# The Mamba stage of a hybrid backbone: GpSimd subtracts a weight tile in four operations instead of one

## The chip, the cores and the metric

One core of a Trainium2 chip runs the kernel. Its engines have queues of their own, worked in order: TensorE (PE; its weight loads are shown apart, as PEld), VectorE (DVE), ScalarE (ACT), GpSimd (POOL) and SyncE (SP), which here issues most transfers. The metric is the time of one execution on the device, in microseconds (us). It was 2333.77 us in the median of three runs (2329.89 to 2337.48).

## The reference

Two layers of a backbone over 512 latent tokens and 256 context tokens of width 1024, all in float32. Layer 0 mixes by differential attention and RWKV-7, layer 1 by a bidirectional Mamba-2; each is followed by a ConvFFN. The change lies in layer 1:

```python
def mamba_inputs(h, w_in, conv_w, conv_b):
    p = h @ w_in
    z, xbc, dt = jnp.split(p, [SSM_INNER, SSM_INNER + SSM_CONV_CH], axis=-1)
    xbc = jax.nn.silu(dwconv_centred(xbc, conv_w, conv_b))
    xs, bm, cm = jnp.split(xbc, [SSM_INNER, SSM_INNER + SSM_GROUPS * SSM_STATE], axis=-1)

def odd_mixer(...):
    for d in range(2):                       # forwards and backwards
        h_ctx_final = ssd_state(...)         # the context's state
        yl, _ = ssd_scan(..., h_ctx_final)   # in chunks of 128 tokens
        y_l = y_l + (jnp.flip(yl, axis=1) if d == 1 else yl)
    o_lat = mamba_out(y_l, z_l, norm_w, w_out)   # gate, group norm, @ w_out
```

## The kernel before

A matrix product is made with three matmuls, on operands split into a high and a low half: with `w = wh + wl` and `x = xh + xl`, PE adds up `wh*xh`, `wh*xl` and `wl*xh`. Activations are split once; weights are split as they come. A weight tile is 128 x 1024 values: SP loads it into `ws`, ScalarE copies it to `wh` in PE's format, and another engine forms `wl = ws - wh`. In most stages that engine is DVE (L150); in the Mamba stage it is POOL (`wsplit_g`, L1349), 52 times. `ws`, `wh` and `wl` have two buffers each.

`dense_stream` (L1433) makes the products of the stage item by item: `item_z`, `item_x`, `item_b`, `item_c` with 8 blocks of 128 inputs each, and `item_o` (the output projection) with 4 blocks of 256 columns. `mm_half` (L1408) makes one half of an item's matmuls, into a PSUM tile `dps`; between the halves the next item is split and the one after it loaded, so a tile is split half an item to an item ahead of its use. After the first half of the next item the result is taken out of PSUM (`evac`): for x, b and c the convolution's five taps and SiLU (`conv_silu`, tiles `cv`, `xf`, `bf`, `cf`), for z a SiLU (`sz`), for o the addition to `xl`. ScalarE and DVE do that.

In turn with the dense stream, `scan(u)` (L1568) makes the recurrence for 4 heads at a time, `u` from 0 to 7. DVE forms the weighted inputs `xw`, which PE multiplies (L1615, L1628) into chunk states `hst`. For each head a tile `bc` with the running sums of the decay is loaded, in ScalarE's queue; POOL masks it with two selects (`mask_bc`, L1557), ScalarE takes the exponential, DVE adds the two directions and multiplies by `cb` (`bc<-bc`, `bc<-bc,cb`), and PE multiplies the result with the inputs (L1668). `fin` (L1671) puts the parts together on DVE (`th`, `gy`) and sums the squares for the group norm in `sqs`, on POOL or DVE by turns (L1686); PE adds these up over partitions (L1732). Before the scans, `dt_chain` (L1453) prepares step sizes and decays from [128, 384] tiles (`e_`, `z`, `dg`).

The framework sets each engine's order from the order of the code, with the results' way out of PSUM raised in priority; it puts the waits in, from what each operation reads and writes.

Of the kernel before, what the change touches and what calls it, by code (L numbers as in the profile page):

```python
# [8 lines left out]
F32 = mybir.dt.float32  # L9
# [116 lines left out]
def build(tc, a, out, dump=None, stop=None):  # L126
    nc = tc.nc
    V, S, G, PE, SY = nc.vector, nc.scalar, nc.gpsimd, nc.tensor, nc.sync
# [4 lines left out]
    def act(o, i, func, bias=0.0, scale=1.0, **kw):  # L133
        S.activation(out=o, in_=i, func=func, bias=bias, scale=scale, **kw)  # L134
# [18 lines left out]
    MUL, ADD, SUB, MAX, MIN = ALU.mult, ALU.add, ALU.subtract, ALU.max, ALU.min  # L153

    with ExitStack() as es:
# [34 lines left out]
        def wload(src, k, m):  # L190
            w = wsp.tile([128, 8, 128], F32, tag="ws", name="ws", bufs=WB[0])
            SY.dma_start(out=w[:, 0:k, 0:m], in_=src.rearrange("(k p) m -> p k m", p=128))
            return w[:, 0:k, 0:m]
# [163 lines left out]
        with ExitStack() as e0:  # L357
# [11 lines left out]
            with ExitStack() as e1:  # L369
# [3 lines left out]
                with tc.tile_pool(name="px", bufs=1) as px:  # L373
# [14 lines left out]
                    for k0 in range(0, KD, 2):  # L388
# [5 lines left out]
                        if k0 in FW:  # L394
                            for m in FW[k0]:
                                w = wload(a["ev_w_in"][:, m * 128:(m + 1) * 128], KD, 128)
# [160 lines left out]
                for j in JA:  # L557
                    q = j // 4
# [713 lines left out]
        with ExitStack() as e3:  # L1272
# [50 lines left out]
            with ExitStack() as e:  # L1323
# [19 lines left out]
                def wsplit_g(w):  # L1343
                    hi = wsp.tile([128, 8, 128], F32R, tag="wh", name="wh", bufs=2)
                    lo = wsp.tile([128, 8, 128], F32R, tag="wl", name="wl", bufs=2)
                    hi = hi.rearrange("p k m -> p (k m)").rearrange("p (k m) -> p k m", m=w.shape[-1])
                    lo = lo.rearrange("p k m -> p (k m)").rearrange("p (k m) -> p k m", m=w.shape[-1])
                    act(hi, w, AF.Copy)
                    G.tensor_tensor(out=lo, in0=w, in1=hi.bitcast(F32), op=SUB)  # L1349
                    return hi, lo  # L1350

                def wload_g(src, k, m):
# [75 lines left out]
                def split_item(it):  # L1428
                    if it is not None and "w" not in it:
                        load_item(it)  # L1430
                        it["w"] = wsplit_g(it["raw"])
# [462 lines left out]
```

## Time and profile before

The profile is of one execution, of 2334.5 us around a span of 2332.8 us. A window of the trace gives the time in which each engine was busy in a stretch; PE's clock is the share of full speed that was granted.

| stretch | length | PE | DVE | ACT | POOL | PE's clock |
|---|---|---|---|---|---|---|
| whole span | 2332.8 us | 2165.8 | 1398.6 | 989.7 | 390.9 | 0.97 |
| up to the stage, 0 to 1400 us | 1400.0 us | 1296.4 | 781.8 | 601.7 | 184.1 | 0.96 |
| the Mamba stage, 1400 to 1935 us | 535.0 us | 487.1 | 423.6 | 253.3 | 189.7 | 0.97 |
| after it | 397.8 us | 382.3 | 193.1 | 134.7 | 17.2 | 0.99 |

A row of the timeline gives the start in the span, the length, the engine, the line, the operation with the tile that it writes and those that it reads, and in brackets the idle time of the engine before it and what ended it. A row of the waits gives the total, the number and the longest. A row of the groups gives count, busy time and mean length in ns, then the idle time before.

### The profile page before, as it was taken

To read this page: it belongs to the slowest core of one execution; us is meant where nothing else is said; L and a number is where in the kernel's file an instruction comes from. 1 tells how busy PE (TensorE), PEld (TensorE's weight loads), DVE (VectorE), ACT (ScalarE), POOL (GpSimd) and SP (SyncE) were. 2 spreads that over 40 slices of the span, in tenths; PEclk is the share of its full clock that TensorE was granted. 3 is DMA by queue.
4 is the path that set the end of the run, shared out by engine and by line. 5 is a ranking of instruction groups with operands and counts; after the bars stand their busy time and mean duration, and the time that the engine had idled before them with its cause. 6 is when DMAs were issued, how large, how long until landed. Compare 5 with 4: busy or idle time off the path is not lost. (4 is left out here: it accounts for less than half of the span.)

```text
span 2332.8 us, 38148 instructions
## 1 busy us (share of the span) xinstructions
PE 2165.8 (93%) x15388; PEld 1931.3 (83%) x15388; DVE 1398.6 (60%) x2510; ACT 989.7 (42%) x1865; POOL 390.9 (17%) x398
## 2 busy tenths in 40 slices
PE   6999998688879899999999998899998988999998
PEld 5989987476768799999999987788887867888887
DVE  4777737847686563333323467987777876444445
ACT  4655537464843342212212245554534534323233
POOL 2000006343510020000000013334324333000000
PEclk9999999799979999999999999999999999999999
DMA  8111222676455512222222213334334322333332
GB/s 279 41 53 50 90 88 82 215 220 207 143 174 161 186 37 64 64 64 64 64 64 64 75 46 84 107 113 115 103 105 110 94 72 73 99 92 99 99 95 86
DMA packets 315760, 241.51 MB, mean 104 GB/s; under 512 B 9920, under 2 KB 273984, under 8 KB 315584
## 3 DMA queue, kind: packets, MB, share of 16 engines
q1 hardware_dynamic: 302272, 213.91, 30.4%
q10 hardware_dynamic: 13312, 25.17, 4.0%
q8 instruction: 121, 1.98, 0.4%
q14 instruction: 55, 0.45, 0.1%
HBM read 222.52 MB, written 16.52 MB: 102 GB/s over the span
## 5 line engine op out<-in xcount | busy, mean ns | idle before, releaser
L134 ACT ACTIVATE wh<-ws 128x1024 fp32r<-128x1024 f32 x196 | 207.5, 1059 | 561.2 <-PE dps L208 471.0
L208 PE MATMUL dps<-hh,wl 128*128 128x384 f32 (+1 forms) x1368 | 399.6, 351 | 1.3 <-DVE wl L150 1.3
L208 PE MATMUL dps<-hl,wh 128*128 128x384 f32 (+1 forms) x1368 | 399.6, 351 | 0.0
L208 PE MATMUL dps<-hh,wh 128*128 128x384 f32 (+1 forms) x1368 | 397.4, 351 | 1.2 <-ACT vT L134 0.9
L150 DVE TENSOR_TENSOR wl<-ws,wh 128x1024 fp32r<-128x1024 f32 x136 | 166.8, 1226 | 203.6 <-ACT wh L134 191.4
L208 PEld LDWEIGHTS dps<-hh,wh 128*128 128x128 f32 x1368 | 250.2, 189 | 15.5 <-ACT vT L134 1.3
L208 PEld LDWEIGHTS dps<-hh,wl 128*128 128x128 f32 x1368 | 250.5, 189 | 15.2 <-DVE wl L150 1.6
L208 PEld LDWEIGHTS dps<-hl,wh 128*128 128x128 f32 x1368 | 250.8, 189 | 14.0 <-issue 0.3
L1349 POOL TENSOR_TENSOR wl<-ws,wh 128x1024 fp32r<-128x1024 f32 x52 | 129.5, 2493 | 224.5 <-ACT wh L134 193.6
L1421 PE MATMUL dps<-hh,wh 128*128 128x384 f32 (+1 forms) x448 | 146.8, 379 | 13.1 <-DVE sz L146 6.5
L1421 PE MATMUL dps<-hl,wh 128*128 128x384 f32 (+1 forms) x448 | 141.9, 368 | 0.0
L1421 PE MATMUL dps<-hh,wl 128*128 128x384 f32 (+1 forms) x448 | 141.0, 366 | 0.0
L146 DVE SCALAR_TENSOR_TENSOR cv<-dps,cwh,cv 128x511 f32<-128x511 f32 (+3 forms) x176 | 109.6, 623 | 25.0 <-ACT cv L134 23.0
L208 PE MATMUL dps<-ah,wh 128*128 128x384 f32 (+1 forms) x384 | 114.8, 352 | 0.0
L208 PE MATMUL dps<-ah,wl 128*128 128x384 f32 (+1 forms) x384 | 114.8, 352 | 0.0
L208 PE MATMUL dps<-al,wh 128*128 128x384 f32 (+1 forms) x384 | 114.7, 352 | 0.0
L137 DVE TENSOR_TENSOR fg<-fg,dps 128x768 f32<-128x768 f32 (+1 forms) x44 | 36.1, 821 | 129.1 <-PE dps L208 126.4
L1421 PEld LDWEIGHTS dps<-hh,wh 128*128 128x128 f32 x448 | 84.0, 195 | 25.7 <-issue 10.2
L134 ACT ACTIVATE bc<-bc,nbt 128x128 f32<-128x128 f32 x256 | 81.5, 392 | 40.8 <-POOL bc L1557 40.1
L146 DVE SCALAR_TENSOR_TENSOR fg<-dps,par,fg 128x511 f32<-128x511 f32 (+1 forms) x132 | 85.1, 658 | 15.2 <-ACT fg L134 12.9
L146 DVE SCALAR_TENSOR_TENSOR x<-dps,mod,x 128x256 f32<-128x256 f32 (+1 forms) x56 | 31.9, 594 | 102.2 <-PE dps L208 100.2
L1421 PEld LDWEIGHTS dps<-hh,wl 128*128 128x128 f32 x448 | 85.1, 194 | 7.0
(432 smaller groups left out, 4452.4 us busy)
## 6 DMA issues: line engine op xcount, KB each, us to landing
aws<-in_ada_w SPq DMA_DIRECT2D x96, 512.0 KB, 5.1
ws<-in_ffn_w_up SPq DMA_DIRECT2D x88, 512.0 KB, 3.8
ws<-in_ssm_w_in SPq DMA_DIRECT2D x40, 512.0 KB, 4.0
ws<-in_ffn_w_down SPq DMA_DIRECT2D x32, 512.0 KB, 4.1
bc<-cumd ACTq DMA_DIRECT2D x32, 512.0 KB, 5.9
ws<-in_ev_w_in SPq DMA_DIRECT2D x26, 512.0 KB, 4.0
th<-ecd ACTq DMA_DIRECT2D x32, 256.0 KB, 4.4
ws<-in_ssm_w_out SPq DMA_DIRECT2D x16, 512.0 KB, 3.5
```

What stands on the lines that cost most here:

```text
L134: S.activation(out=o, in_=i, func=func, bias=bias, scale=scale, **kw)
L137: V.tensor_tensor(out=o, in0=x, in1=y, op=op)
L146: V.scalar_tensor_tensor(out=o, in0=x, scalar=s, in1=y, op0=op0, op1=op1)
L150: eng.tensor_tensor(out=lo, in0=src, in1=hi.bitcast(F32), op=ALU.subtract)
L208: PE.matmul(ps[:, po:po + hi - lo], lhsT=w[:, k0 + k, :], rhs=x[:, xk0 + k, lo:hi], start=(first and k == 0 and j == 0), stop=(last and k ...
L1349: G.tensor_tensor(out=lo, in0=w, in1=hi.bitcast(F32), op=SUB)
L1421: PE.matmul(ps[:, po:po + hi - lo], lhsT=w[:, k, :], rhs=x[:, k, lo:hi], start=(k == 0 and j == 0), stop=(k == KD - 1 and j == 2))
```

## The change

`wl = ws - wh` of one tile is formed by four operations of POOL on a quarter of the tile each: of two blocks where the tile has eight, and of one where it has four. All 52 tiles of L1349 go that way, so 208 operations take the place of 52. ScalarE's copy to `wh`, the loads, the buffers and the matmuls stay.

```diff
                     act(hi, w, AF.Copy)
-                    G.tensor_tensor(out=lo, in0=w, in1=hi.bitcast(F32), op=SUB)
+                    q = w.shape[1] // 4
+                    for k in range(0, 4 * q, q):
+                        G.tensor_tensor(out=lo[:, k:k + q], in0=w[:, k:k + q], in1=hi[:, k:k + q].bitcast(F32), op=SUB)
                     return hi, lo
```

PE, DVE, ACT and SP issue the same operations in the same order as before. On POOL each `wl` becomes four. These are rows of POOL's queue before, at 1619 us of the span, where a select of `bc` stands behind a `wl`:

```order
L1557 AFFINE_SELECT bc<-bc 128x512
L1686 TENSOR_TENSOR sqs<-sqs,th 128x512 [waits DMAHW1_49,DMAHW0_49,Activation_49]
L1349 TENSOR_TENSOR wl<-ws,wh 128x1024 [waits DMAHW1_49,PE_49,Activation_49]
L1557 AFFINE_SELECT bc<-bc 128x512 [waits DMAHW5_49,DVE_49]
L1557 AFFINE_SELECT bc<-bc 128x512
```

and the same place now (the lines have moved by two):

```order
L1559 AFFINE_SELECT bc<-bc 128x512
L1688 TENSOR_TENSOR sqs<-sqs,th 128x512 [waits DMAHW1_49,DMAHW0_49,Activation_49]
L1351 TENSOR_TENSOR wl<-ws,wh 128x256 [waits DMAHW1_49,PE_49,Activation_49]
L1351 TENSOR_TENSOR wl<-ws,wh 128x256 x3
L1559 AFFINE_SELECT bc<-bc 128x512 [waits DMAHW5_49,DVE_49]
L1559 AFFINE_SELECT bc<-bc 128x512
```

The first quarter has the waits of the whole tile, the other three have none, and the selects stand behind all four. At two places of the scan an addition to `sqs` now stands between quarters of the `wl` that it followed.

On PE, the rows of the first item of the dense stream before, where a matmul of `wl` waits for POOL once a tile:

```order
L1421 MATMUL dps<-hh,wh 128x512 [waits DVE_49,Activation_49]
L1421 MATMUL dps<-hl,wh 128x512
L1421 MATMUL dps<-hh,wl 128x512 [waits Pool_49]
L1421 MATMUL dps<-hh,wh 128x512
L1421 MATMUL dps<-hl,wh 128x512
L1421 MATMUL dps<-hh,wl 128x512
L1421 MATMUL dps<-hh,wh 128x512
L1421 MATMUL dps<-hl,wh 128x512
L1421 MATMUL dps<-hh,wl 128x512
```

and now:

```order
L1423 MATMUL dps<-hh,wh 128x512 [waits DVE_49,Activation_49]
L1423 MATMUL dps<-hl,wh 128x512
L1423 MATMUL dps<-hh,wl 128x512 [waits Pool_49]
L1423 MATMUL dps<-hh,wh 128x512
L1423 MATMUL dps<-hl,wh 128x512
L1423 MATMUL dps<-hh,wl 128x512
L1423 MATMUL dps<-hh,wh 128x512
L1423 MATMUL dps<-hl,wh 128x512
L1423 MATMUL dps<-hh,wl 128x512 [waits Pool_49]
```

A matmul of `wl` waits at the start of every quarter, so 156 more matmuls have such a wait: 114 at L1421, 36 at L1414 and 6 at L1854. Some of the copies to `wh` and loads of `ws` wait for one semaphore more than before; their places stay.

## The prediction

> **What bounds the kernel now.** I read the page's busy shares first, then the stage in which the changed line runs (1400 to 1935 us, from the first to the last `wl` of L1349) as one window, then who waits for whom in it.
>
> ```profile
> PE 2165.8 (93%) x15388; PEld 1931.3 (83%) x15388; DVE 1398.6 (60%) x2510; ACT 989.7 (42%) x1865; POOL 390.9 (17%) x398
> 1400.00:1935.00 535.00, 487.10 (x2648) 420.45 (x2646) 423.64 (x645) 253.28 (x524) 189.66 (x127) 0.97 0.36 101
> POOL wl L1349 <- ACT wh L134: 193.6, 32, 14.6
> PEld dps L1854 <- POOL wl L1349: 0.8, 1, 0.8
> ```
>
> The kernel is bound by TensorE (PE), 93% busy over the whole and 487.1 of 535 us in the stage: 47.9 us of idle PE is all that the change can win there, beside the clock (below). GpSimd (POOL) is busy 189.7 us of 535 and waits 193.6 us for ScalarE's `wh`: its own speed bounds nothing. The longest that PE's weight loads wait for a `wl` is 0.8 us, once, so an earlier first quarter of a tile is worth about 1 us at most. Whom PE does wait for is VectorE (DVE), which is 423.6 of 535 us (79%) busy here:
>
> ```profile
> PE sps L1628 <- DVE xw L137: 6.2, 5, 2.1
> PE rsps L1628 <- DVE xw L137: 2.2, 2, 1.4
> PE rsps L1615 <- DVE xw L137: 1.8, 2, 1.1
> PE sps L1615 <- DVE xw L137: 1.2, 2, 0.7
> PE rsps L1732 <- DVE sqs L1686: 3.5, 2, 2.2
> PE sps L1732 <- DVE sqs L1686: 2.9, 2, 2.6
> PE sps L1668 <- issue: 3.5, 2, 2.5
> 1426.40 2.63 DVE L146 SCALAR_TENSOR_TENSOR e__13377<-e__13377,z 128x384 f32<-128x384 f32 x1
> 1429.84 0.98 PE L1421 MATMUL dps<-hh,wh 128*128 128x384 f32 x2 [4.56 <-DVE cv L146]
> ```
>
> Added up, PE waits 11.4 us for `xw`, 6.4 for `sqs`, 3.5 at L1668 (whose operand is DVE's product `bc`) and 4.6 for one `cv`, queued on DVE behind the `e_` at 1426.40: 25.9 us, 54% of the idle time.
>
> **Why DVE is late.** The same operation on DVE has two lengths, and the page's groups mix them.
>
> ```profile
> L137 DVE TENSOR_TENSOR th<-th,rsps 128x512 f32<-128x512 f32 x16 | 10.9, 681 | 7.1 <-PE rsps L1658 7.1
> L137 DVE TENSOR_TENSOR bc<-bc,cb 128x512 f32<-128x512 f32 x32 | 40.0, 1254 | 0.4
> L137 DVE TENSOR_TENSOR bc<-bc 128x512 f32<-128x512 f32 x32 | 32.2, 1014 | 26.6 <-ACT bc L134 21.3 <-POOL bc L1557 4.0 <-issue 1.3
> 1661.15 2.40 POOL L1349 TENSOR_TENSOR wl<-ws,wh 128x1024 fp32r<-128x1024 f32 x1 [0.55 <-POOL bc L1557]
> 1661.18 2.92 DVE L137 TENSOR_TENSOR bc<-bc,cb 128x512 f32<-128x512 f32 x1
> 1664.02 0.68 DVE L137 TENSOR_TENSOR th<-th,sps 128x512 f32<-128x512 f32 x1
> ```
>
> A product of 512 values with one operand in PSUM takes 681 ns. With both in SBUF the means of two such groups are 1254 and 1014, though as many values are read. The timeline says why: `bc` started 0.03 us after a `wl` of POOL, and ended at 1664.10, 0.55 us after that `wl` ended at 1663.55. It stood still for the whole of POOL's operation, 2.92 - 0.68 = 2.24 us, and then ran. The two groups hold 32 x (573 + 333) ns = 29 us of such excess. Counted by operation, 35 DVE operations that read SBUF alone began inside a `wl` and were held, the first and the last of them being
>
> ```profile
> 1419.40 1.86 DVE L141 TENSOR_SCALAR e__13377<-z 128x384 f32<-128x384 f32 x1
> 1926.36 1.04 DVE L150 TENSOR_TENSOR wo<-ws,wo 128x512 fp32r<-128x512 f32 x1
> ```
>
> and their excess over their own undisturbed form sums to 55 us, 1.6 us each: 13% of DVE's busy time.
>
> The Trainium skill, "SBUF — State Buffer", section "Who interferes with whom", states this as a rule: a DVE operation with two SBUF inputs and a GpSimd operation that reads SBUF take a shared port as a lock for a whole instruction, and the second blocks. The 2.92 us agree with it.
>
> **What the change removes and adds.** The lock is now taken in four pieces. What one piece takes is bounded by POOL's subtraction of the same form and of 256 values (L150), and by the time of the selects for whether the port passes on between two queued POOL operations:
>
> ```profile
> 1402.57 0.74 POOL L150 TENSOR_TENSOR hl<-nu,hh 128x256 fp32r<-128x256 f32 x1 [1.51 <-ACT hh L134]
> L150 POOL TENSOR_TENSOR hl<-nu,hh 128x256 fp32r<-128x256 f32 x20 | 16.9, 846 | 28.8 <-ACT hh L134 28.5
> L1349 POOL TENSOR_TENSOR wl<-ws,wh 128x1024 fp32r<-128x1024 f32 x52 | 129.5, 2493 | 224.5 <-ACT wh L134 193.6 <-PE sps L1658 11.0 <-issue 8.8
> 1450.83 2.40 POOL L1349 TENSOR_TENSOR wl<-ws,wh 128x1024 fp32r<-128x1024 f32 x1 [5.21 <-ACT wh L134]
> 1451.52 2.53 DVE L146 SCALAR_TENSOR_TENSOR bf<-bf,cv 128x768 f32<-128x768 f32 x1 [1.51 <-ACT bf L134]
> 1453.24 3.08 POOL L1557 TENSOR_SCALAR_AFFINE_SELECT bc<-bc 128x512 f32<-128x512 f32 x4
> ```
>
> *POOL.* Four undisturbed quarters are 4 x 0.74 = 2.96 us for 2.40, so +0.56 us a tile and +29 us over 52 tiles; at the mean of 846 ns it is +47 us. Both lie in the 345 us in which POOL is idle in this stage.
>
> *DVE.* At 1453.23 a `wl` ended, a select was issued behind it at once, and the waiting `bf` of DVE ended at 1454.05, 0.82 us after the `wl`: DVE got the port first, not the queued select. If it goes so between quarters too, a held operation waits for the rest of one quarter, at most about 0.6 us for up to 2.3. What that returns depends on what DVE does next. Where the next operation reads PSUM (after 1661.18 it is `th<-th,sps`), the other quarters run beside it and about 1.2 of 1.6 us come back. Where it is one more SBUF pair, the next quarter holds that one, and nothing comes back:
>
> ```profile
> 1831.48 2.25 DVE L137 TENSOR_TENSOR bc<-bc,cb 128x512 f32<-128x512 f32 x1
> 1833.65 2.76 DVE L137 TENSOR_TENSOR xw<-xt,wds 128x256 f32<-128x256 f32 x8
> ```
>
> Of the 35, 21 are of the first kind and 14 of the second. 21 x 1.2 + 14 x 0.3 = 29 us, 0.53 of 55. The bounds are 0 (the port is never passed on) and 0.75 (every operation waits a quarter instead of the whole).
>
> *PE.* Of the 25.9 us of waits behind such operations, 0.53 is **13.7 us**, the first term.
>
> *The clock.* After some of the longer gaps the granted clock halves:
>
> ```profile
> 1673.23 1.02 PE L1732 MATMUL rsps<-small,sqs 128*128 128x1 f32 x8 [2.23 <-DVE sqs L1686]
> 1674.70:1678.10 3.40, 3.40 (x13) 3.40 (x12) 2.76 (x8) 3.34 (x6) 1.12 (x2) 0.50 0.08 24
> 1678.20:1681.60 3.40, 3.40 (x23) 3.11 (x23) 1.38 (x2) 2.47 (x4) 1.73 (x1) 1.00 0.00 0
> ```
>
> Behind a gap of 2.23 us PE began 13 matmuls in 3.4 us at a clock of 0.50, and 23 in the next 3.4 us at 1.00. The stage's mean of 0.97 is 0.03 x 535 = 16 us lost. Between none and all of it can come back; where gaps halve, I take 0.4 of it, **6.4 us**.
>
> The Trainium skill, "TensorE: Matmul & The Clock Gate", section "What's actually happening", puts the fall to half speed after at least one idle window of about 3.4 us. Here a gap of 2.23 us was enough, so the measurement decides; by that rule this term would be 0 and the sum some 4 us smaller.
>
> *What is late next.* PE closes a gap and comes earlier to waits that no `wl` feeds (`sz`, `hst` and ScalarE's, the other 46% of its idle time), some of which grow by that much. I keep 0.6 of 13.7 + 6.4 = 20.1 us: **12 us**.
>
> *What it costs.* Each quarter has a semaphore of its own, so 156 matmuls more wait for POOL.
>
> ```profile
> L1421 PE MATMUL dps<-hh,wl 128*128 128x512 f32 x160 | 65.0, 407 | 0.0
> L1421 PE MATMUL dps<-hl,wh 128*128 128x512 f32 x160 | 65.0, 406 | 0.0
> 1619.09 2.39 POOL L1349 TENSOR_TENSOR wl<-ws,wh 128x1024 fp32r<-128x1024 f32 x1
> 1621.44 2.12 POOL L1557 TENSOR_SCALAR_AFFINE_SELECT bc<-bc 128x512 f32<-128x512 f32 x2
> 1622.56 0.70 ACT L134 ACTIVATE bc<-bc,nbt 128x128 f32<-128x128 f32 x2 [2.80 <-POOL bc L1557]
> POOL bc L1557 <- DMA bc<-cumd: 86.8, 19, 12.9
> 1924.47 2.39 POOL wl L1349
> 1926.88 3.55 DMA ws<-in_ssm_w_out
> ```
>
> 20 of the 160 `wl` matmuls waited before, none of the `hl` ones, and the means differ by 1 ns, so 8 ns a wait at most: 0 to 1 us, taken as 0. Selects queued behind a `wl` start later. Mostly they wait for their transfer anyway (86.8 us, 19 times), which covers 0.56 us; not at 1621.44, where ScalarE stood 2.80 us for it and the vector sums behind ScalarE. Such a place loses 0.6 us, or 1.3 with DVE between the quarters; two of them, with the like place one period later, cost **1.1 us** (0 to 3). At the end a weight load waits for the last `wl` but one to free its buffer, on the chain that ended last: **+0.5 us**. The weight loads on SP's queue otherwise follow POOL's last quarter 0.6 us later, inside the wait of ScalarE for PE; where that cover is gone it is 0.6 us a tile.
>
> Sum: 12 - 1.6 = 10.4 us. The profiled execution took 2334.5 us around a span of 2332.8, 0.7 above the median of 2333.77; 2334.5 - 10.4 = 2324.1, and 0.7 less beside the median: **2323 us**.
>
> **The rivals.**
> - *Hidden anyway*, 2327 to 2335 us, 0.22: DVE gets its 29 us back but PE's waits are ended by others. For it speaks that 46% of PE's idle time has no `wl` behind it; against it stand the 25.9 us of rows above. Price: the 0.6 falls to 0.2, 4 - 1.6 = 2.4 us, 2331.
> - *The port is not passed on*, 0.10, slower: the four quarters stand ready together on POOL, and if the next one takes the port before the waiting DVE, a hold lasts the whole 2.96 us instead of 2.40. 35 x 0.56 = 20 us more of DVE, 25.9 / 55 = 0.47 of it on PE, 9.2, and 1.6 of costs: 2344 us. It decides once DVE loses more than about half of the hand-overs. Against it stands `bf` at 1451.52; for it, that no two `wl` here stand back to back with DVE waiting, and that a select is another kind of operation. The Trainium skill, "GPSIMD Engine Reference", section "Instruction dispatch", says that each of the eight cores begins the next instruction when its own share is done, which is how the port might never come free between two; no run so far shows that for two subtractions.
> - *More than forecast*, 2308 us, 0.10: nothing is given back downstream (20.1 us) and half the clock's 16 us more returns with it, 8 - 1.6 = 26.5 in all.
>
> **How the numbers follow.** The forecast, 2316 to 2327, has 0.58. A run can tell about 0.3% from no change, 7 us: under 2326.8 is faster, over 2340.8 slower. Faster takes the forecast and the larger gain, less the forecast's upper edge: 0.66. Slower is the second rival: 0.10. The rest, 0.24, is the same. The range leaves out the far end of both sides: 2306 to 2337.
>
> **What would show it.** In the changed profile the POOL group has 208 operations of 0.74 to 0.85 us; `bc<-bc,cb` falls from 1254 ns to 900 or less and `bc<-bc` from 1014 below 850; DVE's busy time in the stage falls by 25 to 30 us; no DVE operation of 512 values on two SBUF operands lasts over 1.5 us; PE's waits for `sqs` and `xw` halve and the stage's clock is 0.98 or above. The prediction is wrong if DVE's means do not fall (the port stays), or if they fall and PE's idle 47.9 us does not.

## The result and the profile after

| | runs | median | lowest to highest |
|---|---|---|---|
| before | 4 | 2335.62 us | 2329.89 to 2341.77 |
| after | 4 | 2314.75 us | 2309.24 to 2318.11 |

The ratio is 0.9918, with an interval of 0.9889 to 0.9946: 13 to 26 us faster. Two later executions of the kernel before, of 3503 and 5098 us, were in a slower state and are left out of all ratios and means. The profiled execution took 2318.1 us around a span of 2316.4, that is 16.4 less than the one of before.

First the page's busy times, and then the Mamba stage as one window, from the first to the last `wl` as before (the columns are length, PE, PEld, DVE, ACT and POOL, PE's clock, DMA share, GB/s):

```profile
PE 2154.5 (93%) x15388; PEld 1923.4 (83%) x15388; DVE 1370.5 (59%) x2510; ACT 988.8 (43%) x1865; POOL 439.9 (19%) x554
1400.00:1918.00 518.00, 479.86 (x2638) 413.99 (x2637) 394.86 (x642) 251.83 (x522) 239.48 (x282) 0.98 0.37 104
```

The stage is 17.0 us shorter (535 to 518), so the gain lies here. It is made of two parts: PE's idle time fell from 47.9 to 38.1 us (9.8), and its busy time for the same matmuls from 487.1 to 479.9 (7.2), because the clock was 0.98 and not 0.97. DVE's busy time fell by 28.8 us and POOL's rose by 49.8.

The groups of the stage, by shape:

```profile
L1351 POOL TENSOR_TENSOR wl<-ws,wh 128x256 fp32r<-128x256 f32 x208 | 181.3, 901 | 183.4 <-ACT wh L134 163.8 <-issue 14.8 <-PE sps L1660 4.8
L137 DVE TENSOR_TENSOR bc<-bc,cb 128x512 f32<-128x512 f32 x32 | 27.1, 848 | 0.4
L137 DVE TENSOR_TENSOR bc<-bc 128x512 f32<-128x512 f32 x32 | 26.1, 824 | 26.2 <-ACT bc L134 10.9 <-POOL wl L1351 10.2 <-POOL bc L1559 3.6
L137 DVE TENSOR_TENSOR xw<-xt,wds 128x256 f32<-128x256 f32 x80 | 41.0, 566 | 8.0 <-ACT xt L134 8.0
```

The two kinds of `bc` went from 1254 and 1014 ns to 848 and 824. `xw` is the exception, at 566 ns; this is its row of before:

```profile
L137 DVE TENSOR_TENSOR xw<-xt,wds 128x256 f32<-128x256 f32 x80 | 38.9, 539 | 3.7 <-ACT xt L134 3.7
```
The timelines of DVE and of POOL show both cases:

```profile
1475.45 1.14 DVE L137 TENSOR_TENSOR bc<-bc,cb 128x512 f32<-128x512 f32 x1
1476.51 0.68 DVE L137 TENSOR_TENSOR th<-th,sps 128x512 f32<-128x512 f32 x1
1822.29 4.59 DVE L137 TENSOR_TENSOR xw<-xt,wds 128x256 f32<-128x256 f32 x7 [0.58 <-ACT xt L134]
```

```profile
1473.44 2.60 POOL L1351 TENSOR_TENSOR wl<-ws,wh 128x256 fp32r<-128x256 f32 x3
1817.74 7.84 POOL L1351 TENSOR_TENSOR wl<-ws,wh 128x256 fp32r<-128x256 f32 x6
```

At 1475.45 `bc` began inside the last quarter of a tile, and lost 0.46 us (1.14 against 0.68) where it used to lose up to 2.24. At 1822.29 `xw` stand in a row (ten in all, seven in the stretch shown), each reading SBUF alone, while POOL runs quarters. DVE gets the port after one quarter, POOL takes it again for the next, and so on in turn: the first four took 0.94 to 0.98 us in place of 0.41, and the others, behind POOL's last quarter, 0.41 again. Counted by operation, 28 of the stage's 80 `xw` are held now, and 8 were before.

Who PE waits for in the stage (total, number, longest), the rows that answer to those of before:

```profile
PE sps L1630 <- DVE xw L137: 4.4, 7, 2.2
PE rsps L1630 <- DVE xw L137: 3.0, 4, 2.2
PE sps L1617 <- DVE xw L137: 0.9, 2, 0.8
PE rsps L1617 <- DVE xw L137: 0.5, 3, 0.2
PE sps L1734 <- DVE sqs L1688: 1.8, 1, 1.8
PE rsps L1734 <- DVE sqs L1688: 0.2, 1, 0.2
PE sps L1670 <- issue: 2.1, 2, 1.3
PE dps L1423 <- DVE cv L146: 2.5, 2, 1.8
```

For `xw` PE waits 8.8 us (11.4 before), for `sqs` 2.0 (6.4), at L1670 2.1 (3.5), and the longest wait for a `cv` is 1.8 (4.6): 14.7 in place of 25.9. The whole list sums to 43.8 us in place of 53.0, so all other waits grew by 2.0, from 27.1 to 29.1. ScalarE's wait for the selects, as a row of the same view, was 40.1 us before:

```profile
ACT bc L134 <- POOL bc L1559: 46.9, 18, 4.9
```

### The profile page after: what moved, and what is told of

It is laid out like the page before. It is cut to its first block, busy times and chain, and to the rows that moved or that the text cites. A ratio compares the mean times of both kernels' runs of the same rounds, so it can differ in the third digit from the quotient of the medians.

```text
span 2316.4 us, 38339 instructions
## 1 busy us (share of the span) xinstructions
PE 2154.5 (93%) x15388; PEld 1923.4 (83%) x15388; DVE 1370.5 (59%) x2510; ACT 988.8 (43%) x1865; POOL 439.9 (19%) x554
## 5 line engine op out<-in xcount | busy, mean ns | idle before, releaser
L134 ACT ACTIVATE wh<-ws 128x1024 fp32r<-128x1024 f32 x196 | 207.5, 1059 | 555.2 <-PE dps L208 467.1
L150 DVE TENSOR_TENSOR wl<-ws,wh 128x1024 fp32r<-128x1024 f32 x136 | 166.5, 1225 | 203.7 <-ACT wh L134 191.6
L208 PEld LDWEIGHTS dps<-hh,wl 128*128 128x128 f32 x1368 | 250.6, 189 | 15.3 <-DVE wl L150 1.6
L1351 POOL TENSOR_TENSOR wl<-ws,wh 128x256 fp32r<-128x256 f32 x208 | 181.3, 901 | 183.4 <-ACT wh L134 163.8
L146 DVE SCALAR_TENSOR_TENSOR cv<-dps,cwh,cv 128x511 f32<-128x511 f32 (+3 forms) x176 | 109.5, 622 | 29.3 <-ACT cv L134 27.3
L134 ACT ACTIVATE bc<-bc,nbt 128x128 f32<-128x128 f32 x256 | 81.3, 392 | 47.5 <-POOL bc L1559 46.9
```

The source lines that it names most:

```text
L146: V.scalar_tensor_tensor(out=o, in0=x, scalar=s, in1=y, op0=op0, op1=op1)
L150: eng.tensor_tensor(out=lo, in0=src, in1=hi.bitcast(F32), op=ALU.subtract)
L208: PE.matmul(ps[:, po:po + hi - lo], lhsT=w[:, k0 + k, :], rhs=x[:, xk0 + k, lo:hi], start=(first and k == 0 and j == 0), stop=(last and k ...
L1351: G.tensor_tensor(out=lo[:, k:k + q], in0=w[:, k:k + q], in1=hi[:, k:k + q].bitcast(F32), op=SUB)
```

## The experiments

The theory: while POOL's `wl` reads SBUF it holds a port that a DVE operation with two operands in SBUF needs, a held operation waits for the rest of one piece, and the time comes back through PE's waits for DVE and through PE's clock. The rivals: what counts is that a tile's first quarter is there earlier; or that POOL waits for `wh` differently; or that DVE's total time is what counts, wherever it is spent.

Six numbers are compared, each from one profile of a kernel. The *stage* is here the time from the last matmul of the step sizes to the first one of the ConvFFN, so it holds the same work in each. *Gaps* are the stretches of over 60 ns in it in which PE runs neither a matmul nor a weight load, *half clock* is the time in it for which the trace's record of the granted clock shows 0.5, *rest* is the stage less gaps and half of half clock. *Holds* are DVE's operations lengthened by a `wl` (two of the 80 with four pieces, one of the 36 before, fall to whole tiles of L150 at the stage's end, 2.0 us each).

| kernel | ratio, interval | stage | gaps | half clock | rest | DVE busy | holds |
|---|---|---|---|---|---|---|---|
| before | 1 | 564.5 | 52.4 | 34.1 | 495.0 | 444.6 | 36, 57.1 us |
| before, again | | 566.9 | 54.0 | 37.5 | 494.1 | 443.6 | 36, 56.9 |
| two pieces | 0.9973, 0.9956 to 0.9989 | 556.5 | 47.6 | 27.3 | 495.3 | 430.5 | 61, 46.7 |
| **four (the change)** | 0.9918, 0.9889 to 0.9946 | 547.9 | 43.3 | 17.1 | 496.0 | 417.7 | 80, 33.0 |
| four, again | | 548.5 | 41.4 | 23.9 | 495.1 | 418.3 | 84, 34.1 |
| four, reversed | 0.9926, 0.9904 to 0.9949 | 549.3 | 40.3 | 27.3 | 495.4 | 418.1 | 83, 33.8 |
| eight | 0.9916, 0.9898 to 0.9934 | 551.9 | 38.3 | 37.5 | 494.9 | 412.1 | 106, 27.4 |
| eight, again | | 549.9 | 42.0 | 23.9 | 496.0 | 411.7 | 106, 27.5 |
| sixteen | 0.9966, 0.9949 to 0.9983 | 559.9 | 47.7 | 44.4 | 490.0 | 414.2 | 114, 26.4 |
| sixteen, again | | 556.4 | 50.5 | 27.3 | 492.3 | 414.4 | 108, 27.2 |
| memset | 0.9785, 0.9761 to 0.9810 | 516.1 | 20.7 | 10.2 | 490.2 | 389.6 | 3, 4.7 |
| memset, wait kept | 0.9782, 0.9764 to 0.9800 | 514.8 | 20.9 | 6.8 | 490.6 | 389.6 | 7, 5.3 |
| on DVE | 0.9929, 0.9901 to 0.9958 | 555.2 | 45.1 | 44.4 | 487.9 | 446.7 | 2, 3.8 |

The rest is 494 to 496 us in all kernels of up to eight pieces, so there the stage is told by two numbers, gaps and clock. What lies ahead of the stage is the same code in all, and took 1401 to 1423 us from profile to profile; spans are therefore not compared.

**The first quarter earlier.** The four quarters are formed from the last to the first, so that a tile's first block is there last. All else stands.

```diff
-                    for k in range(0, 4 * q, q):
+                    for k in reversed(range(0, 4 * q, q)):
```

> The four quarters of each wl tile are formed from the last to the first, so that the first matmul of wl waits for the quarter that POOL forms last, as it waited for the whole tile in the kernel before. All engines issue the same operations in the same order as in the changed kernel. Theory (the shared port is held for a shorter time): the time stays that of the changed kernel, 0.992 of the kernel before (0.989 to 0.995), and bc<-bc,cb keeps its mean of 848 ns. Rival (PE gains because the first quarter is there earlier): the gain is gone, 0.998 to 1.002 of the kernel before.

Measured 2314.36 us, 0.9926; `bc<-bc,cb` at 859 ns. The gain is the same with the first block last, so PE did not gain from having it early. That rival falls.

**The size of a piece.** Two of 512 values, and eight of 128:

```diff
-                    q = w.shape[1] // 4
-                    for k in range(0, 4 * q, q):
+                    q = w.shape[1] // 2
+                    for k in range(0, 2 * q, q):
```

> Two operations of 512 values a tile. POOL's own subtraction of 512 values takes 1.28 us, so a hold lasts up to 1.1 us where the whole tile gave 2.3 and a quarter 0.6. Theory: between the two, 0.994 to 0.997 of the kernel before, bc<-bc,cb at 950 to 1050 ns, DVE's busy time in the stage 10 to 20 us under that of the kernel before. Rival (what counts is that the port is passed on at all): all of the gain, 0.992.

```diff
-                    q = w.shape[1] // 4
-                    for k in range(0, 4 * q, q):
-                        G.tensor_tensor(out=lo[:, k:k + q], in0=w[:, k:k + q], in1=hi[:, k:k + q].bitcast(F32), op=SUB)
+                    m = w.shape[-1] * w.shape[1] // 8
+                    for k, c in [(k, c) for k in range(w.shape[1]) for c in range(0, w.shape[-1], m)]:
+                        G.tensor_tensor(out=lo[:, k, c:c + m], in0=w[:, k, c:c + m], in1=hi[:, k, c:c + m].bitcast(F32), op=SUB)
```

> Eight operations of 128 values a tile. From POOL's 0.74, 1.28 and 2.40 us for 256, 512 and 1024 values, 128 should take about 0.47, and a tile 3.8 us. Theory: holds of 0.35 us at most, bc<-bc,cb under 800 ns, but POOL 40 us busier than with four and the selects behind a tile 0.8 us later: 0.989 to 0.994 of the kernel before. Rival (every hand-over costs DVE a wait of its own, so more of them cost more): slower than with four, 0.994 to 0.999, with xw<-xt,wds longer than its 566 ns.

The groups with two pieces, then with eight:

```profile
L1351 POOL TENSOR_TENSOR wl<-ws,wh 128x512 fp32r<-128x512 f32 x104 | 147.0, 1435 | 209.5 <-ACT wh L134 190.6 <-PE rsps L1660 6.3 <-PE sps L1660 6.3
L137 DVE TENSOR_TENSOR bc<-bc,cb 128x512 f32<-128x512 f32 x32 | 33.4, 1045 | 0.4
```

```profile
L1351 POOL TENSOR_TENSOR wl<-ws,wh 128x128 fp32r<-128x128 f32 x416 | 225.8, 578 | 158.4 <-ACT wh L134 150.1 <-issue 8.1
L137 DVE TENSOR_TENSOR bc<-bc,cb 128x512 f32<-128x512 f32 x32 | 24.9, 782 | 0.4
```

`bc<-bc,cb` goes 1254, 1045, 848, 782 ns with one, two, four and eight pieces, DVE's busy time 444.6, 430.5, 417.7, 412.1. Two pieces bring a third of the gain (2327.85 us), four nearly all that cutting brings; eight (2312.80) cannot be told from four. Each cut makes more holds and shorter ones: 36 of 1.6 us, 61 of 0.77, 80 of 0.41, 106 of 0.26.

**The port taken away.** POOL writes zeros to the tile, twice, in place of the subtraction. This leaves out the low half of these weights; PE multiplies as before. (A few operations change their order, since `wl` no longer waits for `wh`.)

```diff
-                    q = w.shape[1] // 4
-                    for k in range(0, 4 * q, q):
-                        G.tensor_tensor(out=lo[:, k:k + q], in0=w[:, k:k + q], in1=hi[:, k:k + q].bitcast(F32), op=SUB)
+                    pass
+                    for _ in range(2):
+                        G.memset(lo.bitcast(F32), 0.0)
```

> POOL fills each wl tile with zeros by two memsets of 1024 values in place of the subtraction: the low half of these weights is left out of the product. POOL writes as much as before and reads nothing; the matmuls stay. A few operations change places with their neighbours on PE, DVE and ACT. Theory (DVE is held by what POOL reads): the holds inside wl go altogether, bc<-bc,cb falls to 680 to 720 ns, DVE's busy time in the stage is 45 to 55 us under the kernel before, and the time is 0.980 to 0.990 of it. Rival 1 (any POOL operation holds DVE): bc<-bc,cb stays above 1100 ns and the time at 0.997 to 1.003. Rival 2 (PE's waits are ended by others, and the changed kernel has had all that there is): 0.991 to 0.994.

In the second form the first 64 values are still subtracted, so that POOL waits for `wh` as before, and 960 are zeroed twice (again the low half is left out):

```diff
-                    q = w.shape[1] // 4
-                    for k in range(0, 4 * q, q):
-                        G.tensor_tensor(out=lo[:, k:k + q], in0=w[:, k:k + q], in1=hi[:, k:k + q].bitcast(F32), op=SUB)
+                    G.tensor_tensor(out=lo[:, 0, 0:64], in0=w[:, 0, 0:64], in1=hi[:, 0, 0:64].bitcast(F32), op=SUB)
+                    lf = lo.rearrange("p k m -> p (k m)").bitcast(F32)
+                    G.memset(lf[:, 64:1024], 0.0), G.memset(lf[:, 64:1024], 0.0)
```

> As in the run with memsets, but POOL also subtracts the first 64 values of each tile: that small operation waits for ScalarE's copy and for the load, and frees their buffers, as the whole subtraction did. The low half of the other 960 values is left out. It tells whether the run with memsets was fast because POOL read nothing or because its filling waited for nobody. Theory (reading): holds of 0.2 to 0.3 us, bc<-bc,cb under 740 ns, 0.978 to 0.983 of the kernel before. Rival (the missing wait for ScalarE and the earlier load): 0.987 to 0.993, as with four or eight pieces.

The groups of the first, then of the second:

```profile
L1351 POOL MEMSET wl<- 128x1024 f32 x104 | 99.0, 954 | 260.5 <-PE dps L1423 209.8 <-PE dps L1416 47.4 <-PE dps L1145 0.9
L137 DVE TENSOR_TENSOR xw<-xt,wds 128x256 f32<-128x256 f32 x80 | 32.6, 460 | 10.6 <-ACT xt L134 10.4
L137 DVE TENSOR_TENSOR bc<-bc,cb 128x512 f32<-128x512 f32 x32 | 22.8, 715 | 0.4
```

```profile
L1349 POOL TENSOR_TENSOR wl<-ws,wh 128x64 fp32r<-128x64 f32 x52 | 21.9, 420 | 19.6 <-ACT wh L134 19.1
L137 DVE TENSOR_TENSOR bc<-bc,cb 128x512 f32<-128x512 f32 x32 | 22.9, 717 | 0.4
```

2283.81 and 2286.71 us, 0.9785 and 0.9782. POOL works 1.9 us a tile in operations of 0.95 us, longer than a quarter, and holds DVE no more: `bc<-bc,cb` takes 715 ns. So the holds come from POOL's reading of SBUF, and not from its being busy, nor from its wait for `wh`. The Trainium skill, "SBUF — State Buffer", section "Who interferes with whom", says so: a DVE operation with two SBUF inputs contends with a GpSimd instruction that reads SBUF, not with one that only writes it. The two rows of 715 and 717 ns agree. The kernel is some 50 us, 2.2%, faster without holds: 31.7 by the gaps, 12.0 by the clock, and about 5 by the rest (the second form's, too, is 490.6). What lowers the rest is not shown: sixteen pieces, below, have a rest of 490.0 and 492.3 with PE, DVE and ScalarE in the order of before. PE multiplies zeros here, and whether that bears on its clock was not separated; the holds do not depend on it. The change brings back 0.8%.

**The subtraction on DVE.** POOL does nothing for these tiles, and DVE subtracts each whole.

```diff
                     for k in range(0, 4 * q, q):
-                        G.tensor_tensor(out=lo[:, k:k + q], in0=w[:, k:k + q], in1=hi[:, k:k + q].bitcast(F32), op=SUB)
+                        pass
+                    tt(lo, w, hi.bitcast(F32), SUB)
```

> The whole subtraction of these 52 tiles is made on DVE instead of POOL. It takes 1.23 us there, 64 us in all, and POOL is left with the selects and few sums. Theory: DVE is rid of the 55 us of holds and has 64 us of work more, so its busy time in the stage is 0 to 15 us over the kernel before; wl also comes later, behind other work in DVE's queue: 1.000 to 1.012 of the kernel before. Rival (it is the contact of the two engines that costs, more than the time): 0.985 to 0.995.

```profile
L137 DVE TENSOR_TENSOR wl<-ws,wh 128x1024 fp32r<-128x1024 f32 x52 | 63.9, 1229 | 27.3 <-ACT wh L134 27.2
L137 DVE TENSOR_TENSOR bc<-bc,cb 128x512 f32<-128x512 f32 x32 | 22.5, 705 | 0.2
```

A miss. DVE is as busy as before the change (446.7 against 444.6 us: 63.9 us of own work in place of the holds), as expected, and yet the kernel took 2319.53 us, 0.9929, which lies in the range of the rival (it is the contact of the two engines that costs). PE's gaps are 45.1 us, near those of four pieces. But the scheduler also put PE's, ScalarE's and DVE's operations into another order here (the rest is 487.9 us, not 495). Whether that order, the place of the 1.2 us operations or the missing contact brought the gain was not separated, so this run does not decide between DVE's total and the holds. The kernel of sixteen pieces, next, bears on it with the order of before.

**Smaller still.** Sixteen pieces of 64 values (in the diff of eight, 16 in place of 8), twice, with the changed kernel and that of eight pieces beside them:

> Sixteen operations of 64 values a tile. A piece of 64 took 0.32 us, of 128 0.46, of 256 0.74, so a tile takes 16 x 0.32 less the overlap, some 4.6 us, and POOL is busy some 50 us more than with eight pieces. Theory with a turning point: holds by wl stay near the 27 us of eight pieces (each one shorter, but more of them), while wl and the selects behind it come 1 us later still; 0.992 to 0.997 of the kernel before, no better than four. Rival (the shorter the better as long as POOL has idle time): 0.987 to 0.991.

> The kernel of sixteen pieces once more, to see whether holds over many pieces come back. If the port is sometimes passed from one GpSimd subtraction to the next, as the first profile of sixteen pieces shows (two `th` of 5.2 and 4.7 us over undisturbed 0.68), this profile has at least one VectorE operation of 512 values held for over 2 us by `wl` alone, and the mean of th<-th lies above 900 ns. If those two were an accident of that execution, no `wl` holds an operation for over 0.9 us and th<-th lies at 760 to 800 ns, as with eight pieces. Time 2318 to 2340 us either way.

> The changed kernel once more, for its profile. From the wl of the first tile on, the stage was 495 us plus PE's idle time plus half of the time at half clock, in every profile of the two kernels and of two, four and eight pieces. Here too it should be 495 within 2. PE's idle time should be 40 to 44 us (52 and 54 in two profiles of the kernel before), and the time at half clock anything from 17 to 31 us (34 and 38 before).

> The kernel of eight pieces once more. The first theory (a hold is the rest of one piece) gives th<-th of 760 to 800 ns, bc<-bc,cb of 770 to 810 and no hold by `wl` alone over 0.9 us. If the port is now and then kept over many pieces as soon as the pieces are short, a hold of over 1.5 us by `wl` alone shows here too. TensorE's gaps in the stage 36 to 42 us, its time at half clock 15 to 40 us, and the rest of the stage 495 us within 2.

Sixteen gave 2327.62 us, 0.9966: most of the gain is lost again. The groups of its second profile, and the timelines of DVE and of POOL in it:

```profile
L1351 POOL TENSOR_TENSOR wl<-ws,wh 128x64 fp32r<-128x64 f32 x832 | 307.7, 406 | 113.9 <-ACT wh L134 99.0 <-issue 14.9
L137 DVE TENSOR_TENSOR th<-th 128x512 f32<-128x512 f32 x32 | 31.1, 972 | 0.7
```

```profile
1601.56 4.81 DVE L137 TENSOR_TENSOR th<-th 128x512 f32<-128x512 f32 x1
...
1680.54 3.57 DVE L137 TENSOR_TENSOR gl<-gy,gh 128x512 fp32r<-128x512 f32 x1
...
1733.40 3.79 DVE L137 TENSOR_TENSOR th<-th 128x512 f32<-128x512 f32 x1
```

```profile
1600.95 6.33 POOL L1351 TENSOR_TENSOR wl<-ws,wh 128x64 fp32r<-128x64 f32 x19
...
1679.87 3.69 POOL L1351 TENSOR_TENSOR wl<-ws,wh 128x64 fp32r<-128x64 f32 x13
...
1731.75 6.36 POOL L1351 TENSOR_TENSOR wl<-ws,wh 128x64 fp32r<-128x64 f32 x19
```

Here DVE loses hand-overs: at 1601.56 a `th` of 0.68 us stood still for 4.1, until POOL's pieces were almost through. The first profile has two such operations (5.20 and 4.66 us), this one three; the two profiles of four pieces and the two of eight have none, and `th<-th` takes 972 ns here and 772 with eight pieces. DVE's busy time is no more than with four (414.4 us), but the gaps are 47.7 and 50.5 us, not 42: DVE's total is not by itself what they go by.

The granted clock of every run is on record, and what it lacks of 1, times the span, is about what the clock cost (half clock within a gap counts in it too; each mean below is uncertain by some 2 us):

| kernel | runs | mean clock | clock's cost | mean time less this cost |
|---|---|---|---|---|
| before, beside the next two | 17 | 0.9671 | 76.9 us | 2257.9 us |
| four, reversed | 6 | 0.9705 | 68.3 | 2247.6 |
| eight | 6 | 0.9710 | 67.1 | 2246.7 |
| before, beside sixteen | 15 | 0.9660 | 79.3 | 2255.9 |
| sixteen | 12 | 0.9651 | 81.2 | 2246.5 |

Sixteen pieces keep the 9 to 11 us that come without the clock, and lose the clock's 9 to 10. Their two profiles have six and four gaps of over 3 us in the stage; the eight profiles of up to eight pieces have at most one each. Whether the long holds made these gaps is open: POOL is at 307.7 us of its time in these pieces, so selects and sums behind them start later as well.

The profile of four pieces again (2324.88 us) shows the gaps, 41.4, and the rest, 495.1, as expected. That of eight again (2311.19) has no hold by these pieces over 0.7 us, as the first theory has it.

**The best of these.** Eight pieces, and GpSimd's other subtractions (L150) in pieces of 128 values too:

```diff
-        eng.tensor_tensor(out=lo, in0=src, in1=hi.bitcast(F32), op=ALU.subtract)
+        if eng is not V and len(src.shape) == 3:
+            for k in range(src.shape[1]):
+                eng.tensor_tensor(out=lo[:, k], in0=src[:, k], in1=hi[:, k].bitcast(F32), op=ALU.subtract)
+            return
+        n = src.shape[-1] if eng is V else 128
+        for k in range(0, src.shape[-1], n):
+            sl = (slice(None),) * (len(src.shape) - 1) + (slice(k, k + n),)
+            eng.tensor_tensor(out=lo[sl], in0=src[sl], in1=hi[sl].bitcast(F32), op=ALU.subtract)
```

> Eight pieces a tile in the Mamba stage, and the subtractions that POOL makes at the seams of the other stages (L150: 8 weight tiles, 4 half tiles, 32 pieces of activations) in pieces of 128 values too. In the kernel before DVE loses some 26 us to POOL ahead of the stage, mostly not to L150, and 5.7 us behind it, nearly all to L150 with nacc on the chain that ended last. Theory: 2 to 5 us better than eight pieces alone, 0.988 to 0.992 of the kernel before. Rival (the seams wait for their weights, which come later in pieces): 0.992 to 0.996.

2309.42 us, 0.9880 (0.9857 to 0.9904), the fastest that computes all of the result. The holds by L150's whole tiles after the stage are gone: DVE's `nacc<-nacc,nsq`, held for 2.0 us twice in the changed kernel, takes 528 ns in the mean there, not 741. Its interval overlaps that of eight pieces, so the last step is not certain.

**Before, again**, for how far one profile of the same kernel lies from another:

> The kernel before once more, for its profile. It tells how much of the time at half clock belongs to the kernel and how much to one execution: 34 us of half clock in the first profile of the kernel before (first wl to the FFN's matmuls), 17 and 27 with four pieces, 27 with two, 38 with eight. If the clock's share of the gain is real, it shows 30 us or more; if it is chance, anything from 17 to 38. PE's idle time there should be 52 us again, within 4, in either case.

2348.65 us; the stage within 2.4 us of the first, and most of the difference ahead of it (1422.8 us, not 1411.6). Half clock is 37.5 us, over the 30 that a real share of the clock was to show; but one profile of eight pieces has 37.5 as well, so it is the clocks of all runs, above, that show the share.

## Why the prediction was right, and which term was off

The forecast was 2323 us (2316 to 2327) and faster; the median was 2314.75, a little beyond its fast edge. Its own steps:

- **The lock is taken in pieces, and DVE gets it between them: right.** `bc<-bc,cb` at 848 ns (forecast 900 or less), `bc<-bc` at 824 (below 850), and no operation of 512 values on two SBUF operands over 1.5 us, the longest being a `gl` of 1.26. Zeros in place of the subtraction, with POOL busy all the same, show that it is POOL's reading that holds DVE.
- **29 us of DVE's time come back: right, a little high.** The stage's DVE time fell by 26.9 us, 0.49 of the 55. The step that takes little back where SBUF pairs follow each other was the one that bites: held `xw` went from 8 to 28. PE's waits for `xw` therefore did not halve (11.4 to 8.8 us); those for `sqs` did (6.4 to 2.0).
- **13.7 us of PE's waits: high.** The same four waits gave back 11.2.
- **The clock, 6.4 us: somewhat low.** PE's busy time fell by 7.2 us. Over two profiles of each kernel half clock goes from 35.8 to 20.5 us, worth 7.7; but eight pieces had 37.5 in one profile and 23.9 in the next, so a single profile says little of this term. By the clocks of all runs it is 9 to 10 us with four reversed and eight pieces, about half of the gain; the four runs of the change have a mean clock of 0.9710, as eight pieces. The prediction's alternative of 0 for this term passes over a gap of its own rows, the 4.56 us at L1421, which is longer than the 3.4 us that it names.
- **"I keep 0.6 of 13.7 + 6.4": this step failed.** It gave up 8.1 us of 20.1, for waits that grow as PE comes earlier. Those waits grew by 2.0 us, and the clock's part came back in full. What was kept is 9.8 of idle time and 7.2 of clock, 17.0 us with all costs in it, where the sum had 12 less 1.6. The two profiles of each kernel say the same: the stage went from 565.7 to 548.2 us, by 17.5.
- **Costs of 1.6 us: not seen apart.** The rest went from 494.6 to 495.6 us in the means of two, no more than two profiles of one kernel differ by. ScalarE's waits for the selects grew, as feared, by 6.8 us in all (40.1 to 46.9), and yet PE's wait at L1670, behind that work, fell from 3.5 to 2.1.
- **Quarters of 0.74 to 0.85 us: low.** The group's mean is 901 ns, since a quarter also waits for the DVE operation that took its turn: the first of the three at 1473.44 took 1.23, beside a `bc` that had begun just before it.

Of the rivals, *hidden anyway* fell with the idle time. *More than forecast* had its first half (nothing given back downstream) come nearly true, and of its second, 8 us more of the clock, some 3. *The port is not passed on* fell for quarters: a hold was 0.41 us in the mean. Its mechanism is real all the same, and showed with pieces of 64 values, at 2 or 3 operations a run. The Trainium skill's rule that was weighed for it ("GPSIMD Engine Reference", section "Instruction dispatch": each core begins the next instruction when its own share is done) would let such holds come at every size; the rows show them only at 64 values, and for the larger pieces the measurement decides.

## What to carry to other kernels

Where an operation of VectorE shows two lengths, lay its long cases beside GpSimd's timeline: a GpSimd operation that reads SBUF holds it to its end, so cut GpSimd's work into pieces about as long as the VectorE operations beside it, or shorter (256 values at 0.74 us or 128 at 0.46 here, beside operations of 0.41 to 0.68), and try how short: with 64 values most of the gain was gone. Count what follows a held operation: one that reads PSUM lets the time come back, a row of SBUF pairs is held once per piece. And when a wait on the bounding engine shrinks, take a discount only as large as the waits that stand right behind it, and none on the clock: here they were 2.0 us and nothing, and the discount 8.1. Read the clock's part from many runs, not from one profile.

## What was not expected of the hardware

- The stage is 495 us plus PE's gaps plus half of its time at half clock, within 1 us over eight profiles of up to eight pieces whose gaps went from 38 to 54 us and half clock from 17 to 37. It is no rule: sixteen pieces, with the same order of work on PE, DVE and ScalarE, gave 490 and 492.
- The clock halves in steps that differ from run to run of one kernel: half clock in the stage was 37.5 and 23.9 us with eight pieces, 44.4 and 27.3 with sixteen. In the prediction's rows a gap of 2.23 us came ahead of one such stretch. In the thirteen profiles of the table each stretch at half clock lasts 3.41 us, or two or three times that. In the first of the kernel before, the eight stretches stand behind gaps of 2.02 to 4.53 us, while gaps of 2.08 and 2.18 us have none behind them; what decides is open.
- GpSimd's subtraction, undisturbed, took 0.32, 0.46, 0.74, 1.30 and 2.40 us for 64, 128, 256, 512 and 1024 values: 0.18 us plus 2.17 ns a value.
- VectorE and GpSimd take turns at the port by whole operations, and with pieces of 64 values VectorE can miss over ten turns in a row (4.1 us). What sets which operation misses is open.
- Not only pairs of SBUF operands are held. The `e_<-z` of the prediction's rows has one operand of 384 values, began inside a `wl` and took 1.86 us; this operation of the same form, with no `wl` beside it, took 0.36:

```profile
1414.24 0.36 DVE L141 TENSOR_SCALAR z<-e__13377 128x384 f32<-128x384 f32 x1
```
